# Summed weight tiles of a seven-product matmul: both of their transfers on GpSimd's queue, three units ahead

## The chip, the cores and the metric

The kernel runs on one core of one Trainium2 chip. The time is device microseconds of one execution. Three timed runs of the kernel before took 825.82, 832.07 and 833.29 us (median 832.07); a separate execution was recorded by the hardware profiler. Engines are named as in the profile: PE is TensorE (PEld its weight loads), DVE is VectorE, ACT is ScalarE, POOL is GpSimd, SP is SyncE, which issues most transfers.

## The reference

One layer of a decoder trunk on 256 tokens of width 2048, all in float32. What matters here is the order of the matrix products:

```
h  = rmsnorm(x)
u  = h @ w_in          # 12288 columns: conv fields, recurrence fields, then gates ga and gb (2048 columns each)
ya = short_conv(u);  yb = gated_recurrence(u)
m  = sigmoid(ga) * (ya @ w_a_out) + sigmoid(gb) * (yb @ w_b_out)
x  = x + m @ w_o
x  = x + sigmoid(rmsnorm(x) @ w_ple_gate) * (p @ w_ple_proj)
out = rmsnorm(x)
```

## The kernel before

Weights stream from DRAM once. Every weight tile (128 x 1024, two blocks of 512 columns) is cut into a high part (ScalarE copies it to float32r, line 160) and a low part (VectorE subtracts, line 161); a product is three matmuls, high by high, high by low, low by high (`triple`, lines 1021 to 1025). The main loop (line 1087 on) goes through a list of items, one per weight tile: projections of p, the fields of w_in, then for j = 0 to 3 the gate columns followed by four tiles each of w_a and w_b, then w_o, then the last gate. Items are split `LEAD` = 3 or more ahead of their matmuls and loaded `AHEAD` = 4 ahead; raw tiles have three buffers of two items each. Epilogues are generators of which each item advances one step.

For j = 1, 2, 3 the columns of ga and of gb, with two token halves and two halves of a 256-row chunk, form 2 x 2 block products. Of the eight chunks c, those in `SEVEN` (0, 2, 3, 5, 6) are done with seven products in place of eight (Strassen's scheme in Winograd's form); these are items of kind "S", called S units here (S0, S2, S3, S5, S6). Chunks 1, 4 and 7 are done plainly, as two items of kind "C" each. An S unit needs sums of weight blocks beside the blocks themselves:

- sA: the tile of ga (two blocks), which is also cut into whi and wlo and used as it is;
- sB: the second block of the tile of gb;
- sT: the tile of gb plus the first blocks of both tiles, added by the DMA engines: a plain load of the tile of gb (SP's queue, line 142) and then a load with `accum_op=add` (GpSimd's queue, line 143), which waits for the first.

`combine_weights` (line 176), called two items before the unit, adds sT and sB into sA on VectorE (line 691, twice) and cuts sT, sB and sA into thi/tlo, bhi/blo and thi/tlo. ScalarE's order for a unit is whi, thi (sT), bhi, thi (sA). thi and tlo have three buffers, bhi and blo one; sA, sB and sT have two each. `unit_products` (line 1050) issues the 21 matmuls, in the order x by the two halves of sA, then bhi/blo, then the summed weights. The sums on the token side are made once by `token_sums` (line 725), in three steps from w_a of j = 0 on, in scratch tiles `t4`.

All these lie in the pool "st", opened (`second_part`, line 967) with the scratch pool "tmp2" after the last gate item of j = 0, and closed when w_a of j = 3 begins (`parked`, line 1096). Then `unpark` (line 780) loads three stored tiles m into a pool "back" and cuts them; `ep_bb` (line 764) makes m for each j.

The order of instructions on each engine is the program's, with epilogue steps held behind the newest split; the queues of SP and of GpSimd are in order, and an issue that waits for a buffer or a transfer holds those behind it.

Of the kernel before, what the change touches and what calls it, by code (L numbers as in the profile page):

```python
# [9 lines left out]
F32 = mybir.dt.float32  # L10
F32R = mybir.dt.float32r
AF = mybir.ActivationFunctionType
ALU = mybir.AluOpType
PSUM = bass.MemoryType.PSUM

P = 128
# [7 lines left out]
CW = 512  # L24
# [23 lines left out]
def hybrid_kernel(ctx, tc, xT, x, pT, prm, gfin, masks, w_in, w_a, w_b, w_o, w_pg, w_pp, out):  # L48
    nc = tc.nc
# [9 lines left out]
    pools, closers = {}, {}  # L59
# [13 lines left out]
    state = {"tmp": "tmp1"}  # L73
# [3 lines left out]
    def nm(s):  # L77
        uid[0] += 1
        return f"{s}_{uid[0]}"

    def t4(tag="t4", bufs=None):
        bufs = bufs or {"tmp1": 8, "tmp2": 2, "tmp3": 5}[state["tmp"]]
        return pools[state["tmp"]].tile([P, 1024], F32, tag=tag, bufs=bufs, name=nm(tag))

    def bank(tag):
# [7 lines left out]
    loaded = {}  # L93
    parts = {}
    sums = {}

    groups = [("PP", j, w_pp, j, "pT") for j in range(4)]
    for n, (kind, j) in enumerate(IN_ORDER):
# [6 lines left out]
    items = []  # L105
    for gi, (kind, j, w, g, op) in enumerate(groups):
        if kind == "gb" and SEVEN[j]:
            continue
        for c in range(w.shape[2]):
            it = {"gi": gi, "kind": kind, "j": j, "c": c, "last": c == w.shape[2] - 1}  # L110
# [11 lines left out]
    def raw_of(pos):  # L122
        it = items[pos]
        if it["raw"] not in loaded:
            if it["kind"] == "S":
                t = tuple(
                    pools["st"].tile([P, n, CW], F32, tag=tag, bufs=2, name=nm(tag))
                    for tag, n in (("sA", 2), ("sB", 1), ("sT", 2))
                )
            else:  # L130
                t = wp.tile([P, 2, 2 * CW], F32, tag="raw", bufs=3, name=nm("raw"))
            loaded[it["raw"]] = t
        return loaded[it["raw"]]

    def load(pos):
        it = items[pos]
        if it["raw"] not in loaded:
            raw, (w, g, c) = raw_of(pos), it["w"]
            if it["kind"] == "S":
                A, B, X = raw  # L140
                for to, n, z in ((X, 1, 0), (A, 0, 0), (B, 1, 1)):
                    nc.sync.dma_start(out=to.rearrange("p n x -> p (n x)"), in_=w[g + n, :, c, z * CW :])
                nc.gpsimd.dma_start(  # L143
                    out=X, in_=w[g : g + 2, :, c, :CW].rearrange("n p x -> p n x"), accum_op=ALU.add
                )
            elif it["kind"] == "C":
                for n in range(2):
                    nc.sync.dma_start(out=raw[:, n, :], in_=w[g + n, :, c, :])
            elif pos < APART:
                for i in range(2):  # L150
                    w, g, c = items[pos + i]["w"]
                    nc.sync.dma_start(out=raw[:, i, :], in_=w[g, :, c, :])
            else:
                nc.sync.dma_start(out=raw, in_=w[g, :, c : c + 2, :])

    def pair_of(pool, n, tags=("whi", "wlo"), width=2 * CW):
        return tuple(pool.tile([P, width], F32R, tag=tag, bufs=n, name=nm(tag)) for tag in tags)

    def cut(hi, lo, src):
        a = nc.scalar.activation(out=hi, in_=src, func=AF.Copy)  # L160
        v = nc.vector.tensor_tensor(out=lo, in0=src, in1=hi.bitcast(F32), op=ALU.subtract)  # L161
        state["splits"] = (a.ins, v.ins)
# [12 lines left out]

    def combine_weights(pos):
        st = pools["st"]
        A, B, X = raw_of(pos)
        add(A[:, 0], X[:, 0], B[:, 0])
        add(A[:, 1], A[:, 0], A[:, 1])  # L180
        ts = []
        for n, src in enumerate((X, B, A)):
            hi, lo = pair_of(st, 1, ("bhi", "blo"), CW) if n == 1 else pair_of(st, 3, ("thi", "tlo"))
            cut(hi, lo, src.rearrange("p n x -> p (n x)"))
            ts += [(hi[:, i * CW : (i + 1) * CW], lo[:, i * CW : (i + 1) * CW]) for i in range(1 if n == 1 else 2)]
        t1, t3, b22, t2, t4_ = ts
        sums[pos] = (b22, t1, t3, t2, t4_)

    last_group = len(items) - w_pg.shape[2]
    gate = len(items) - 4 * w_pg.shape[2]  # L190
# [88 lines left out]
    def blocks(ap):  # L279

        return ap.rearrange("p (c b e) -> p c b e", b=4, e=32)
# [8 lines left out]
    def to_dram(src, tag, bufs):  # L290
        d = dram.tile([P, 4, T], F32, tag=tag, bufs=bufs, name=nm(tag))
        to = d.rearrange("(b i) a x -> a i b x", b=4)
        for a in range(4):
            nc.sync.dma_start(out=to[a], in_=src[32 * a : 32 * a + 32, :].rearrange("i (b x) -> i b x", b=4))
        return d
# [6 lines left out]
    def turned(src, lag, dst=None):  # L302
        d = to_dram(src, "turn", 3)
        yield
        nc.sync.dma_start(out=src, in_=d.rearrange("p a x -> p (a x)"))
        for _ in range(lag):
            yield
        dst = t4() if dst is None else dst
        square_turn(dst, src)
        return dst  # L310
# [379 lines left out]
    def add(out, a, b):  # L690
        nc.vector.tensor_tensor(out=out, in0=a, in1=b, op=ALU.add)  # L691
# [33 lines left out]
    def token_sums():  # L725
        nu = len(SEVEN[1])
        state["S"] = pair_of(pools["st"], 1, ("shi", "slo"), nu * 4 * P)
        state["S"] = tuple(v.rearrange("p (u s t) -> p u s t", u=nu, s=4) for v in state["S"])
        for first, n in TOGETHER:
            for _ in range(3):  # L730
                yield
            F, S = (t4()[:, : n * 4 * P] for _ in range(2))
            c = SEVEN[1][first]
            hi, lo = (v[:, 2 * c : 2 * (c + n), :] for v in state["hT"])
            Fv = F.rearrange("p (k t) -> p k t", t=T)
            nc.vector.tensor_tensor(out=Fv, in0=hi.bitcast(F32), in1=lo.bitcast(F32), op=ALU.add)
            yield
            Fv = F.rearrange("p (u r b t) -> p u r b t", u=n, r=2, b=2)
            Sv = S.rearrange("p (u s t) -> p u s t", u=n, s=4)
            a11, a12, a21, a22 = Fv[:, :, 0, 0], Fv[:, :, 1, 0], Fv[:, :, 0, 1], Fv[:, :, 1, 1]  # L740
            s1, s2, s3, s4 = (Sv[:, :, i] for i in range(4))
            for out, u, v, op in (
                (s1, a21, a22, ALU.subtract), (s2, s1, a11, ALU.subtract),
                (s3, a11, a21, ALU.subtract), (s4, a12, s2, ALU.add),
            ):
                nc.vector.tensor_tensor(out=out, in0=u, in1=v, op=op)
            hi, lo = (v[:, first : first + n] for v in state["S"])
            nc.scalar.activation(out=hi, in_=Sv, func=AF.Copy)
            nc.vector.tensor_tensor(out=lo, in0=Sv, in1=hi.bitcast(F32), op=ALU.subtract)
            yield  # L750
# [13 lines left out]
    def ep_bb(j, psum):  # L764
        ga, gb = state["ga"], state["gb"]
        for t in range(NT):
            s = slice(t * CW, (t + 1) * CW)
            nc.vector.tensor_tensor(out=gb[:, s], in0=gb[:, s], in1=psum[t], op=ALU.mult)  # L768
        m = t4()
        for t in range(NT):  # L770
            s = slice(t * CW, (t + 1) * CW)
            nc.vector.tensor_tensor(out=spread(m, t), in0=blocks(ga[:, s]), in1=blocks(gb[:, s]), op=ALU.add)
        if j == 3:
            m = yield from turned(m, 3)
            put_m(j, m)
        else:
            state["m", j] = to_dram(m, f"m{j}", 1)
            yield

    def unpark():  # L780
        def back():
            return pools["back"].tile([P, 1024], F32, tag="back", bufs=4, name=nm("back"))

        srcs = []
        for j in range(3):
            if j == 0:
                srcs = [back() for _ in range(2)]
                for i in range(2):
                    nc.sync.dma_start(out=srcs[i], in_=state["m", i].rearrange("p a x -> p (a x)"))
                yield  # L790
                yield
            if j == 2:
                srcs.append(back())
                nc.sync.dma_start(out=srcs[2], in_=state["m", 2].rearrange("p a x -> p (a x)"))
                yield
                yield
            m = back()
            square_turn(m, srcs[j])
            put_m(j, m)
            yield  # L800
# [286 lines left out]
    for pos, it in enumerate(items[:last_group]):  # L1087
        mark = len(nc.cur_bb.bb.instructions)
        kind, j, c, last = (it[n] for n in ("kind", "j", "c", "last"))
        _, _, w, g, opname = groups[it["gi"]]  # L1090
# [42 lines left out]
        if pos == NORM + 4:  # L1133
# [3 lines left out]
            for i in range(4):  # L1137
                z = slice(i * Q, (i + 1) * Q)
# [29 lines left out]
        if pos == begun:  # L1168
            finish()
            second_part()  # L1170
            active.append(token_sums())
        if kind == "O" and j == 0 and c == nch - 3:
            finish()
            third_part()
# [22 lines left out]
    for t, halves in ((0, (0, 1)), (1, (0,)), (1, (1,))):  # L1197
        bk, n = bank("g"), CW // 2
# [91 lines left out]
```

## Time and profile before

| | |
|---|---|
| timed runs, us | 825.82, 832.07, 833.29 |
| profiled execution, us | 828.21 |
| its span, us | 826.4 |
| mean granted TensorE clock | 0.992 |
| DMA traffic | 198.52 MB, mean 240 GB/s |
| q1 (SP's transfers) | 188.93 MB, 65.8% of 16 engines |
| q0 (GpSimd's transfers) | 7.87 MB, 5.6% of 16 engines |

The span runs from the first to the last instruction; the profiled execution's own time is 1.8 us longer. The S units of the three groups lie between about 435 and 615 us. In the profile's tables a row names a line, an engine and an operation with its tiles (out<-in); brackets in a timeline give the idle time before the instruction and what ended it. The windows view gives, for stretches of the span, busy time and number of instructions of each engine, the granted clock, the DMA engines' share and the rate. A landing is the time from a transfer's issue to its completion.

### The profile page before, as it was taken

How to read it: one execution, taken by the hardware profiler on the slowest of the kernel's cores; microseconds unless marked ns; L12 is line 12 of the kernel's file. 1: busy time of each engine (PE TensorE's matmuls, PEld its weight loads, DVE VectorE, ACT ScalarE, POOL GpSimd, SP SyncE). 2: the span in 40 equal slices, each digit the busy share in tenths (PEclk: the TensorE clock that was granted, in tenths of full speed). 3: DMA queues.
4: the chain of work that ended last, by engine and by line, in shares of the span. 5: the costliest groups of instructions: out<-in, count | busy, mean ns of one | idle time of the engine just before them, and what ended most of it. 6: DMA issues, size and time to landing. Idle time of an engine off the chain costs nothing.

```text
span 826.4 us, 10670 instructions
## 1 busy us (share of the span) xinstructions
PE 808.5 (98%) x4059; PEld 666.2 (81%) x4059; DVE 588.6 (71%) x745; ACT 458.6 (55%) x614; POOL 39.7 (5%) x42
## 2 busy tenths in 40 slices
PE   9999999999999999999999989999999999999995
PEld 6888888888888888888888868878877788888885
DVE  6756598767666588758678878688787756676932
ACT  7576466456464575475454555366455455566623
POOL 1000000010000000010000110110100000000210
PEclk9999999999999999999999989999999999999998
DMA  9998555648876555648888986997854888797712
GB/s 335 391 308 299 190 184 198 204 158 273 266 222 233 180 196 192 218 159 290 277 274 248 282 238 224 271 294 245 245 181 194 276 290 282 261 339 283 264 42 102
DMA packets 52659, 198.52 MB, mean 240 GB/s; under 512 B 6784, under 2 KB 16256, under 8 KB 37888
## 3 DMA queue, kind: packets, MB, share of 16 engines
q1 hardware_dynamic: 47952, 188.93, 65.8%
q0 software_dynamic: 4080, 7.87, 5.6%
q10 hardware_dynamic: 576, 1.05, 0.4%
q8 instruction: 31, 0.51, 0.2%
q14 instruction: 20, 0.16, 0.1%
HBM read 184.19 MB, written 13.63 MB: 239 GB/s over the span
## 4 chain that ended last, share of the span: by engine, by line
PE 76%; DVE 10%; DMA 7%; issue 4%; ACT 2%; POOLq 0%; POOL 0%; DVEq 0%; ACTq 0%
PE g L1023 24%; PE g L1024 24%; PE g L1025 24%; DMA sT<-in_w_in 6%; DVE wlo L161 4%; DVE tlo L161 2%; DVE sA L691 2%; ACT whi L160 1%; DMA raw<-in_w_o 1%; PE s L1024 1%; PE s L1025 1%; PE s L1023 1%; PE s L474 1%; DVE gb L768 0%; DVE back L298 0%
## 5 line engine op out<-in xcount | busy, mean ns | idle before, releaser
L161 DVE TENSOR_TENSOR wlo<-raw,whi 128x1024 fp32r<-128x1024 f32 (+1 forms) x264 | 319.9, 1227 | 160.8 <-ACT whi L160 158.9
L160 ACT ACTIVATE whi<-raw 128x1024 fp32r<-128x1024 f32 (+1 forms) x264 | 272.9, 1049 | 209.2 <-PE g L1025 175.4
L1024 PE MATMUL g<-wlo,xh 128*128 128x512 f32 (+1 forms) x738 | 283.7, 384 | 0.0
L1025 PE MATMUL g<-whi,xl 128*128 128x512 f32 (+1 forms) x738 | 283.6, 384 | 0.0
L1023 PE MATMUL g<-whi,xh 128*128 128x512 f32 (+1 forms) x738 | 283.5, 385 | 0.0
L1025 PEld LDWEIGHTS g<-whi,xl 128*128 128x128 f32 x738 | 138.6, 188 | 27.7
L1024 PEld LDWEIGHTS g<-wlo,xh 128*128 128x128 f32 x738 | 138.7, 188 | 27.6
L1023 PEld LDWEIGHTS g<-whi,xh 128*128 128x128 f32 x738 | 138.7, 188 | 27.1
L1024 PE MATMUL g<-wlo,mh 128*128 128x512 f32 x128 | 49.9, 390 | 0.2 <-DVE wlo L161 0.2
L1023 PE MATMUL g<-whi,mh 128*128 128x512 f32 x128 | 49.7, 389 | 0.0
L1025 PE MATMUL g<-whi,ml 128*128 128x512 f32 x128 | 49.5, 389 | 0.0
L160 ACT ACTIVATE thi<-sT 128x1024 fp32r<-128x1024 f32 x15 | 15.8, 1053 | 35.1 <-DMA sT<-in_w_in 35.1
L1024 PE MATMUL s<-wlo,xh 128*128 128x512 f32 x84 | 32.7, 389 | 0.0
L1025 PE MATMUL s<-whi,xl 128*128 128x512 f32 x84 | 32.7, 389 | 0.0
L1023 PE MATMUL s<-whi,xh 128*128 128x512 f32 x84 | 32.5, 391 | 0.0
L1024 PEld LDWEIGHTS g<-wlo,mh 128*128 128x128 f32 x128 | 24.0, 188 | 5.6 <-DVE wlo L161 0.7
L143 POOL DMA_DIRECT2D sT<-in_w_in x15 | 18.2, 1213 | 213.4 <-DMA sT<-in_w_in 69.5
L1023 PEld LDWEIGHTS g<-whi,mh 128*128 128x128 f32 x128 | 24.0, 188 | 5.1
L1025 PEld LDWEIGHTS g<-whi,ml 128*128 128x128 f32 x128 | 24.0, 188 | 5.0
L1024 PE MATMUL g<-wlo,ybTh 128*128 128x512 f32 x64 | 25.0, 391 | 1.0 <-DVE wlo L161 1.0
L160 ACT ACTIVATE thi<-sA 128x1024 fp32r<-128x1024 f32 x15 | 15.8, 1055 | 18.0 <-DVE sA L691 17.9
L1025 PE MATMUL g<-whi,ybTl 128*128 128x512 f32 x64 | 24.9, 389 | 0.0
(214 smaller groups left out, 917.5 us busy)
## 6 DMA issues: line engine op xcount, KB each, us to landing
raw<-in_w_in SPq DMA_DIRECT2D x66, 1024.0 KB, 5.0
raw<-in_w_o SPq DMA_DIRECT2D x16, 1024.0 KB, 7.0
raw<-in_w_pg SPq DMA_DIRECT2D x16, 1024.0 KB, 6.9
raw<-in_w_in SPq DMA_DIRECT2D x28, 512.0 KB, 5.3
raw<-in_w_a SPq DMA_DIRECT2D x8, 1024.0 KB, 7.8
raw<-in_w_b SPq DMA_DIRECT2D x8, 1024.0 KB, 7.0
turn<-t SPq DMA_DIRECT2D x60, 128.0 KB, 2.8
t<-turn SPq DMA_DIRECT2D x15, 512.0 KB, 5.2
```

What stands on the lines that cost most here:

```text
L143: nc.gpsimd.dma_start(out=X, in_=w[g : g + 2, :, c, :CW].rearrange("n p x -> p n x"), accum_op=ALU.add)
L160: a = nc.scalar.activation(out=hi, in_=src, func=AF.Copy)
L161: v = nc.vector.tensor_tensor(out=lo, in0=src, in1=hi.bitcast(F32), op=ALU.subtract)
L474: nc.tensor.matmul(out, X[:, 0, h, s], X[:, 1, h, t], start=True, stop=True, tile_position=(0, i * n))
L691: nc.vector.tensor_tensor(out=out, in0=a, in1=b, op=ALU.add)
L1023: nc.tensor.matmul(psum, oh, hi, start=first, stop=False)
L1024: nc.tensor.matmul(psum, oh, lo, start=False, stop=False)
L1025: nc.tensor.matmul(psum, ol, hi, start=False, stop=last)
```

## The change

Line numbers below are those of the kernel before.

- The plain load of sT leaves `load` (SP's queue) and the adding one goes with it into a new function `add_by_dma`, which issues both on GpSimd's queue for the next S unit that has none yet.
- It is called three times when the pool "st" is open, so that the first three units' transfers are issued there, and once at the end of each `combine_weights`, for the unit three further on. sT has three buffers in place of two.
- To make room, the scratch pool "tmp2" has one t4 in place of two; the token sums use buffers of thi and tlo for their scratch tiles; the m of j = 3 is turned into a tile of the pool "back", which has five buffers in place of four.

In the changed program the order of instructions on TensorE is that of before; on VectorE and ScalarE the order is that of before in the S units, but for tile names and waits. SP has 15 transfers fewer and GpSimd 15 more. GpSimd's list is: three plain loads, three adding ones, and from there in turn one plain load (it waits for VectorE's last read of the buffer) and its adding one (it waits for that load), to the fifteenth unit.

```diff
-        bufs = bufs or {"tmp1": 8, "tmp2": 2, "tmp3": 5}[state["tmp"]]
+        bufs = bufs or {"tmp1": 8, "tmp2": 1, "tmp3": 5}[state["tmp"]]
...
+    pair_sums = {}
...
                 t = tuple(
-                    pools["st"].tile([P, n, CW], F32, tag=tag, bufs=2, name=nm(tag))
-                    for tag, n in (("sA", 2), ("sB", 1), ("sT", 2))
+                    pools["st"].tile([P, n, CW], F32, tag=tag, bufs=2, name=nm(tag)) for tag, n in (("sA", 2), ("sB", 1))
                 )
...
             if it["kind"] == "S":
-                A, B, X = raw
-                for to, n, z in ((X, 1, 0), (A, 0, 0), (B, 1, 1)):
-                    nc.sync.dma_start(out=to.rearrange("p n x -> p (n x)"), in_=w[g + n, :, c, z * CW :])
-                nc.gpsimd.dma_start(
-                    out=X, in_=w[g : g + 2, :, c, :CW].rearrange("n p x -> p n x"), accum_op=ALU.add
-                )
+                for n, to in enumerate(raw):
+                    nc.sync.dma_start(out=to.rearrange("p n x -> p (n x)"), in_=w[g + n, :, c, n * CW :])
...
+    def add_by_dma():
+        pos = next((n for n, it in enumerate(items) if it["kind"] == "S" and n not in pair_sums), None)
+        if pos is not None:
+            w, g, c = items[pos]["w"]
+            X = pair_sums[pos] = pools["st"].tile([P, 2, CW], F32, tag="sT", bufs=3, name=nm("sT"))
+            nc.gpsimd.dma_start(out=X.rearrange("p n x -> p (n x)"), in_=w[g + 1, :, c, :])
+            nc.gpsimd.dma_start(out=X, in_=w[g : g + 2, :, c, :CW].rearrange("n p x -> p n x"), accum_op=ALU.add)
...
     def combine_weights(pos):
         st = pools["st"]
-        A, B, X = raw_of(pos)
+        (A, B), X = raw_of(pos), pair_sums[pos]
...
         sums[pos] = (b22, t1, t3, t2, t4_)
+        add_by_dma()
...
-            F, S = (t4()[:, : n * 4 * P] for _ in range(2))
+            F, S = (
+                pools["st"].tile([P, 2 * CW], F32R, tag=tag, bufs=3, name=nm(tag))[:, : n * 4 * P].bitcast(F32)
+                for tag in ("thi", "tlo")
+            )
...
         if j == 3:
-            m = yield from turned(m, 3)
+            m = yield from turned(m, 3, back())
...
+    def back():
+        return pools["back"].tile([P, 1024], F32, tag="back", bufs=5, name=nm("back"))
+
     def unpark():
-        def back():
-            return pools["back"].tile([P, 1024], F32, tag="back", bufs=4, name=nm("back"))
...
             active.append(token_sums())
+            for _ in range(3):
+                add_by_dma()
```

## The prediction

> **What bounds the kernel now.** I read the page first (busy time, chain of waits, groups), then waits by engine, the windows of 395 to 660 us in 5 us steps, and last the timelines of the five engines there.
>
> ```profile
> span 826.4 us, 10670 instructions
> ...
> PE 808.5 (98%) x4059; PEld 666.2 (81%) x4059; DVE 588.6 (71%) x745; ACT 458.6 (55%) x614; POOL 39.7 (5%) x42
> ...
> PE g L1023 24%; PE g L1024 24%; PE g L1025 24%; DMA sT<-in_w_in 6%; DVE wlo L161 4%; DVE tlo L161 2%; DVE sA L691 2%; ACT whi L160 1%; DMA raw<-in_w_o 1%; PE s L1024 1%; PE s L1025 1%; PE s L1023 1%; PE s L474 1%; DVE gb L768 0%; DVE back L298 0%
> ```
>
> TensorE is busy 98% of the span, so only about 18 us of it are idle. The chain gives 6% (50 us) to transfers of sT, but most of those 50 us lie beside busy matmuls: a late sT first eats the lead that the splits have over TensorE. What counts is where TensorE itself stops.
>
> ```profile
> PE s L1024 <- DVE blo L161: 3.7, 5, 1.0
> PE s L1023 <- ACT bhi L160: 2.7, 1, 2.7
> ...
> ACT thi L160 <- DMA sT<-in_w_in: 35.1, 8, 6.8
> ```
>
> ```profile
> 475.00:480.00 5.00, 1.31 (x5) 0.57 (x4) 3.52 (x5) 3.48 (x5) 1.19 (x1) 0.90 0.59 150
> 480.00:485.00 5.00, 5.00 (x13) 3.84 (x13) 5.00 (x5) 3.31 (x4) 0.00 (x0) 0.50 1.05 327
> ...
> 540.00:545.00 5.00, 4.20 (x18) 3.49 (x19) 4.93 (x7) 3.16 (x5) 0.38 (x1) 1.00 0.98 290
> ...
> 605.00:610.00 5.00, 4.96 (x21) 3.77 (x21) 4.93 (x6) 3.16 (x5) 0.00 (x0) 1.00 0.09 15
> ```
>
> Columns: stretch, then busy us of PE, PEld, DVE, ACT, POOL with counts, granted clock, DMA share, GB/s. TensorE waits for the pieces of an S unit (bhi, blo) 6 times, 3.7 + 2.7 = 6.4 us together, in one place of each of the three seven-product groups (near 475, 540, 605). Each time ScalarE's thi stands behind the summed weights of the fifth or fourth S unit, and bhi, the adds and blo stand behind thi. After the first stop the granted clock is 0.50 for 5 us.
>
> ```profile
> 474.84 0.39 PE L1024 MATMUL s<-wlo,xh 128*128 128x512 f32 x1
> 475.07 0.39 PE L1025 MATMUL s<-whi,xl 128*128 128x512 f32 x1
> 478.15 0.50 PE L1023 MATMUL s<-bhi,shi 128*128 128x512 f32 x1 [2.69 <-ACT bhi L160]
> 479.65 0.79 PE L1024 MATMUL s<-blo,shi 128*128 128x512 f32 x1 [1.00 <-DVE blo L161]
> 480.24 0.63 PE L1025 MATMUL s<-bhi,slo 128*128 128x512 f32 x1
> ...
> 485.79 0.42 PE L1023 MATMUL s<-whi,xh 128*128 128x512 f32 x1
> ```
>
> ```profile
> 539.54 0.39 PE L1023 MATMUL s<-bhi,shi 128*128 128x512 f32 x1
> 540.80 0.50 PE L1024 MATMUL s<-blo,shi 128*128 128x512 f32 x1 [0.87 <-DVE blo L161]
> ```
>
> A matmul normally follows after 0.23 us. From 480.24 to 485.79 there are 13 steps in 5.55 us where 13 x 0.23 = 2.95 would do: 2.6 us lost to the clock. A wait costs a little more than its length: 540.80 - 539.54 - 0.23 = 1.03 us for a wait of 0.87, so 0.16 more; six times, 1.0 us. **All that sT costs the matmuls is 6.4 + 2.6 + 1.0 = 10.0 us**, and this is the most that the change can win at this place.
>
> [...]
>
> **The change part by part.** Now the last sT of group one (unit S6), whose lateness causes the stop:
>
> ```profile
> 454.12 1.22 DVE L161 TENSOR_TENSOR tlo<-sT,thi 128x1024 fp32r<-128x1024 f32 x1
> 459.59 1.22 DVE L161 TENSOR_TENSOR tlo<-sT,thi 128x1024 fp32r<-128x1024 f32 x1
> 460.83 0.33 SPq L142 DMA_DIRECT2D sT<-in_w_in  x1
> 467.60 1.19 POOL L143 DMA_DIRECT2D sT<-in_w_in  x1 [6.87 <-DMA sT<-in_w_in]
> 471.14 1.22 DVE L161 TENSOR_TENSOR wlo<-sA,whi 128x1024 fp32r<-128x1024 f32 x1
> 476.44 0.69 DVE L691 TENSOR_TENSOR sA<-sT,sB 128x512 f32<-128x512 f32 x1 [4.08 <-issue]
> 478.91 0.68 DVE L161 TENSOR_TENSOR blo<-sB,bhi 128x512 fp32r<-128x512 f32 x1
> ```
>
> With two buffers, S6 takes S3's, free when its tlo ends (459.59 + 1.22 = 460.81); SP loads at 460.83, GpSimd adds at 467.60, and VectorE goes on at 476.44 instead of 471.14 + 1.22 = 472.36. With three buffers S6 takes S2's, free at 454.12 + 1.22 = 455.34, 5.5 us earlier. blo ends 478.91 + 0.68 - 476.44 = 3.15 us after the first add begins; unstalled, TensorE would need blo at 475.07 + 2 x 0.23 = 475.53. So **sT must be there by 472.4, 17.1 us after S2's buffer is free**.
>
> The new pair of transfers is the one term that the trace does not show: a plain load on GpSimd's queue, then the adding one, which waits for it.
>
> ```profile
> sT<-in_w_in SPq DMA_DIRECT2D x15, 512.0 KB, 5.5
> ...
> sT<-in_w_in POOLq DMA_DIRECT2D x15, 512.0 KB, 9.3
> ```
>
> The landings of SP's line 142 (sT, sA and sB together), then those of GpSimd's line 143:
>
> ```profile
> DMA to landing us min/median/max: 3.6/6.1/10.5
> ```
>
> ```profile
> L143 POOL DMA_DIRECT2D sT<-in_w_in x15: 1194/1203/1366, 403.8 to 597.3; - x15
> ...
> DMA to landing us min/median/max: 5.9/9.3/11.6
> ```
>
> Load: between SP's 3.6 and 10.5 us; I take 5.5, the median of the same bytes to the same tile. Add: unchanged, 5.9 to 11.6, median 9.3. With 0.5 for the semaphore between, an estimate, the chain takes 15.3 us (bounds 10.0 to 22.6), and S6's sT lands at 455.34 + 15.3 = 470.6, 1.8 us ahead of need. For the other two groups:
>
> ```profile
> 518.88 1.22 DVE L161 TENSOR_TENSOR tlo<-sT,thi 128x1024 fp32r<-128x1024 f32 x1
> ...
> 545.47 0.39 PE L1023 MATMUL s<-bhi,shi 128*128 128x512 f32 x1
> ```
>
> Free at 518.88 + 1.22 = 520.10; need: TensorE's blo at 545.47 - 1.03 + 0.23 = 544.7, less 3.15, is 541.5. That leaves 21.4 us for 15.3; group three repeats group two. S5 has more time still, since its buffer (S0's) comes free a unit pair earlier. So all three stops go: -10.0 us.
>
> GpSimd issues 15 more transfers: 15 x 1.2 = 18 us on an engine busy for 39.7 of 826.4, at nothing. Its queue is in order, so S5's add, waiting for its load, holds back S6's load.
>
> ```profile
> 440.18 1.22 DVE L161 TENSOR_TENSOR tlo<-sT,thi 128x1024 fp32r<-128x1024 f32 x1
> ```
>
> S5's chain starts when S0's tlo ends, 440.18 + 1.22 = 441.40, and its add is out by 441.40 + 5.5 + 0.5 + 1.2 = 448.6, ahead of S6's start at 455.34. If that cover went, S6's chain would start later by the overlap. SP loses 15 x 0.33 = 5 us of issues and its waits before sT; nothing in the chain hangs on SP there.
>
> The first three chains start when the pool is open, near 400, for a need after 435; they move S3's traffic into this stretch:
>
> ```profile
> 395.00:430.00 35.00, 35.00 (x156) 28.98 (x155) 23.21 (x27) 17.52 (x20) 2.58 (x2) 1.00 0.89 289
> ```
>
> The share of 0.89 leaves 11% of 35 us, 3.9 us, and the splits there wait for TensorE and not for weights, so nothing; uncovered, up to one pair's 4.6 us of DMA time (second rival) would meet a lead of three items. The token sums move into thi and tlo buffers, where the same engine writes and reads in order: nothing. One scratch buffer in place of two serves one m per group, stored long before the next: nothing. The fifth `back` buffer makes its loads wait for the last S unit's matmuls; that unit starts near 609 and has 21 x 0.23 = 4.8 us of them. The loads go out after it even now:
>
> ```profile
> 616.45 0.85 SPq L789 DMA_DIRECT2D back<-m  x2
> 627.00 2.60 SPq L154 DMA_DIRECT2D raw<-in_w_o  x2
> ```
>
> What is queued behind them on SP goes at 627: nothing, and up to 10 us later would still be covered. When the stops go, VectorE is late next: blo of S6 then ends at 472.36 + 3.15 = 475.5, just as TensorE comes to it.
>
> **Sum.** The profiled execution took 828.21 us (span 826.4); minus 10.0 is 818.2. It was 3.9 us faster than the median of the runs shown (832.07); from that the same step gives 822.1. I forecast the middle, 820, with a base of 830.
>
> **Rivals.** *Late in group one only.* The margin is 1.8 us. With a chain of 20 us S6 is 2.9 us late, stops TensorE as long as now and halves the clock again (2.9 + 2.6 + 0.2 = 5.7), while groups two and three stay clean: gain 4.3, 826. For it: both bounds' sum is 22.6. Against: the chain's parts are medians. Chance 0.18.
>
> *Moved traffic is no gain.* The pair competes with S6's own sA, issued behind it:
>
> ```profile
> 462.57 0.33 SPq L142 DMA_DIRECT2D sA<-in_w_in  x1
> ```
>
> ```profile
> q1 hardware_dynamic: 13049, 47.00, 61.3%
> q0 software_dynamic: 4080, 7.87, 20.9%
> ```
>
> In 395 to 615 the adds took 20.9% of 220 us over 15, 3.1 us of all engines each, and a plain load 0.52 / 47.00 of 61.3% of 220 us, 1.5 us. sA's own landings:
>
> ```profile
> DMA to landing us min/median/max: 4.1/6.6/8.8
> ```
>
> If an add goes ahead of sA, it lands at 462.57 + 8.8 + 3.1 = 474.5 at worst, TensorE stops as now, and the time stays 830. Against it: by the median alone sA is there at 469.2. Chance 0.10. [...]
>
> *Slower: GpSimd's queue is slower than any row.* If load and add take 24.2 us, S6 is 7.1 late in group one (7.1 + 2.6 + 0.2 = 9.9) and 2.8 late in the other two, each with a halved clock (5.6): 21.1 against 10.0 now, 841. It decides from 22.2 us on (7.9 + 1.0 + 1.0, as now). The longest landings seen make 22.6, so it needs both at their worst in every group. Chance 0.10.
>
> **How the numbers follow.** Forecast 0.62 (820), the rivals 0.18 (826), 0.10 (830), 0.10 (841). A measurement tells about 1% (8.3 us) from no change. Of the forecast's 0.62, whose 10.0 is just above that, three quarters count as faster, and a little of the first rival: 0.49 faster; 0.11 slower, from the last rival; 0.40 within 1%. The range leaves out the slower rival and little at the bottom: 812 (fastest run, 825.82, less 10.0, less another 3.9 by which executions differ) to 831.
>
> **What would show it.** Right: no wait of ScalarE's thi for sT, matmuls without a stop near 475, 540 and 605, clock 1.00 there, GpSimd's load issued right after the tlo of three units before, and a chain of about 15 us. Wrong: a chain over 17 us with TensorE waiting for bhi in the first group; weight loads or sA as the new last arrival; an idle TensorE near 615 to 630 behind `back`.

## The result and the profile after

The changed kernel took 818.19, 818.54, 817.41 and 818.57 us (median 818.37). The kernel before, on the same chip, took 825.82, 832.07, 833.29 and 832.19 (median 832.13). The ratio is 0.9855 with a 95% interval of 0.9811 to 0.9898: faster by about 1.5%, where 820 us had been forecast. The profiled executions are 10.0 us apart, 828.21 before and 818.19 after (spans 826.4 and 816.1, 10.3 apart). The kernel before was run another 37 times in three later sets, with medians of 826.33, 825.77 and 825.94; against those, the gain is 7.4 to 8.0 us. The changed kernel hardly moves (817 to 819 us in all runs), the kernel before does (823 to 834), so most of what is uncertain in the ratio is the kernel before.

The page of the changed kernel, busy time and the chain of work that ended last:

```profile
span 816.1 us, 10646 instructions
...
PE 804.2 (99%) x4059; PEld 664.6 (81%) x4059; DVE 589.0 (72%) x745; ACT 459.1 (56%) x614; POOL 49.2 (6%) x57
...
PE g L1033 26%; PE g L1034 26%; PE g L1032 26%; DVE wlo L165 3%; PE s L1033 2%; PE s L1034 2%; PE s L1032 2%; DMA sA<-in_w_in 1%; DMA raw<-in_w_pp 1%; DVE tlo L165 1%; ACT whi L164 1%; DMA raw<-in_w_o 1%; DVE sA L696 1%; PE s L479 1%; DVE back L303 0%
```

The transfers of sT, 6% of the chain before, are gone from these entries. Of the S units' transfers, sA is there now, with 1%. The waits of 395 to 650 us show the same; each row gives the total, the number and the longest in us:

```profile
POOL sT L158 <- DMA sT<-in_w_in: 86.1, 12, 13.3
...
ACT whi L164 <- DMA sA<-in_w_in: 3.5, 2, 2.7
...
PE s L1033 <- DVE blo L165: 1.1, 1, 1.1
```

ScalarE's thi waited for sT 8 times before (35.1 us) and does not wait for it once now. TensorE's six waits for the pieces of an S unit (6.4 us) have become one of 1.1. The 86.1 us in the first row are GpSimd's: the adding transfer waits for its load, and no engine waits for GpSimd in this stretch. The windows answer to the three of before (us, then busy time of each engine, granted clock, DMA share, GB/s); the later ones are shifted by what has been gained by then:

```profile
475.00:480.00 5.00, 3.86 (x17) 2.91 (x16) 4.97 (x7) 4.04 (x5) 0.00 (x0) 1.00 0.95 242
480.00:485.00 5.00, 5.00 (x23) 4.14 (x23) 4.96 (x6) 1.29 (x2) 1.78 (x2) 1.00 0.84 236
530.00:535.00 5.00, 5.00 (x24) 4.14 (x23) 4.74 (x7) 2.30 (x3) 1.74 (x2) 1.00 0.89 314
535.00:540.00 5.00, 5.00 (x24) 4.14 (x23) 3.69 (x4) 3.71 (x5) 0.04 (x1) 1.00 0.99 230
...
600.00:605.00 5.00, 5.00 (x24) 4.14 (x23) 5.00 (x5) 4.13 (x5) 0.00 (x0) 1.00 0.16 26
```

TensorE is full wherever it stopped before, but for 1.1 us in the first of these rows, and the clock stays at 1.00, after that stop too. Now unit S6 of the first group, the one whose sT was late. Its rows in the timeline of the changed kernel, in order of time (brackets: idle before, and what ended it):

```profile
454.96 1.22 DVE L165 TENSOR_TENSOR tlo<-sT,thi 128x1024 fp32r<-128x1024 f32 x1
456.48 0.60 POOL L157 DMA_DIRECT2D sT<-in_w_in  x1 [7.78 <-DVE tlo L165]
461.36 1.17 POOL L158 DMA_DIRECT2D sT<-in_w_in  x1 [4.28 <-DMA sT<-in_w_in]
462.07 1.05 POOL L157 DMA_DIRECT2D sT<-in_w_in  x1
463.40 0.33 SPq L141 DMA_DIRECT2D sA<-in_w_in  x1
472.09 1.06 ACT L164 ACTIVATE whi<-sA 128x1024 fp32r<-128x1024 f32 x1 [2.70 <-DMA sA<-in_w_in]
472.14 1.18 POOL L158 DMA_DIRECT2D sT<-in_w_in  x1 [9.01 <-DMA sT<-in_w_in]
473.06 1.04 ACT L164 ACTIVATE thi<-sT 128x1024 fp32r<-128x1024 f32 x1
476.13 0.39 PE L1032 MATMUL s<-bhi,shi 128*128 128x512 f32 x1
477.66 0.50 PE L1033 MATMUL s<-blo,shi 128*128 128x512 f32 x1 [1.14 <-DVE blo L165]
```

S2's tlo frees the buffer at 454.96 + 1.22 = 456.18; GpSimd loads at 456.48 and adds at 461.36, and the adding transfer lands 6.9 us later:

```profile
DMA to landing us min/median/max: 6.9/6.9/6.9
```

So sT is whole at 468.3, 12.1 us after its buffer came free, and 4.8 us before ScalarE cuts it at 473.06, without a wait. The last to come is now sA: issued at 463.40, cut at 472.09 after a wait of 2.70. From its cut on, everything of S6 is late by that much less the lead, and TensorE stops once, 477.66 - 476.13 - 0.23 = 1.30 us. Why sA comes so late is the prediction's question asked of another tile: its buffer is the one that S3's sA had, VectorE's last read of that ends at 463.38 (a tlo of 1.22 us from 462.16), and SP issues the load at 463.40. sA has two buffers; a third one was not tried.

### The profile page after: what moved, and what is told of

Read it like the earlier page. It is cut to its first block, busy times and chain, and to the rows that moved or that the text cites. A ratio compares the mean times of both kernels' runs of the same rounds, so it can differ in the third digit from the quotient of the medians.

```text
span 816.1 us, 10646 instructions
## 1 busy us (share of the span) xinstructions
PE 804.2 (99%) x4059; PEld 664.6 (81%) x4059; DVE 589.0 (72%) x745; ACT 459.1 (56%) x614; POOL 49.2 (6%) x57
## 4 chain that ended last, share of the span: by engine, by line
PE 85%; DVE 7%; issue 3%; DMA 3%; ACT 2%; POOLq 0%; POOL 0%; DVEq 0%; ACTq 0%
PE g L1033 26%; PE g L1034 26%; PE g L1032 26%; DVE wlo L165 3%; PE s L1033 2%; PE s L1034 2%; PE s L1032 2%; DMA sA<-in_w_in 1%; DMA raw<-in_w_pp 1%; DVE tlo L165 1%; ACT whi L164 1%; DMA raw<-in_w_o 1%; DVE sA L696 1%; PE s L479 1%; DVE back L303 0%
## 5 line engine op out<-in xcount | busy, mean ns | idle before, releaser
L1032 PE MATMUL g<-whi,yaTh 128*128 128x512 f32 x64 | 24.9, 389 | 0.0
L1033 PE MATMUL g<-wlo,yaTh 128*128 128x512 f32 x64 | 24.9, 389 | 0.0
```

The lines of the kernel that those rows point to most:

```text
L1032: nc.tensor.matmul(psum, oh, hi, start=first, stop=False)
L1033: nc.tensor.matmul(psum, oh, lo, start=False, stop=False)
```

## The experiments

The theory from the prediction: the time hung on the buffer. A third one lets S6's transfers start 5.5 us earlier, and that is the gain; which queue carries the plain load matters little. The rival: the queue matters, because transfers on one queue keep their order (in the trace of the changed kernel S6's add, issued at 461.36, lands at 468.3, and the load of 462.07 behind it on GpSimd's queue at 471.9). A second question came with the profile after: why sA is late there.

All times are the changed kernel's with one edit, unless said otherwise; ratios are to the kernel before, run beside it. Each run left one profiled execution, so a trace is one case and the timed runs say how typical it is.

**Two buffers in place of three, both transfers on GpSimd's queue.**

```diff
-            X = pair_sums[pos] = pools["st"].tile([P, 2, CW], F32, tag="sT", bufs=3, name=nm("sT"))
+            X = pair_sums[pos] = pools["st"].tile([P, 2, CW], F32, tag="sT", bufs=2, name=nm("sT"))
...
-            for _ in range(3):
+            for _ in range(2):
                 add_by_dma()
```

> The changed kernel with two buffers of sT in place of three, and two units ahead in place of three; both transfers stay on GpSimd's queue. Buffer theory (the third buffer lets the pair of transfers start one unit sooner, and this is the gain): the last unit's pair starts only when the third unit's tlo ends, some 5 us later, the stops of TensorE near 475, 540 and 600 us come back at least in part, 822 to 829 us. Queue theory (what counts is that the plain load no longer stands in SP's queue): no stop, 818 us as with three buffers.

Measured: 833.51 us (828.09 to 836.15), ratio 1.0067 (1.003 to 1.0104). That is beyond the 822 to 829 of the buffer theory. In the trace the stops of the first two groups are back and longer: TensorE loses 5.26 + 1.44 us near 481 and 3.40 + 1.44 near 551, and the clock is halved (0.50 in 480 to 485; 0.986 in the mean of the execution, where the changed kernel had 0.997); the third group has no stop. In the timeline of this kernel, the buffer's release, S5's add, S6's load, S6's add and the cut:

```profile
459.50 1.22 DVE L165 TENSOR_TENSOR tlo<-sT,thi 128x1024 fp32r<-128x1024 f32 x1
460.05 1.18 POOL L158 DMA_DIRECT2D sT<-in_w_in  x1 [3.90 <-DMA sT<-in_w_in]
461.01 0.81 POOL L157 DMA_DIRECT2D sT<-in_w_in  x1
471.38 1.17 POOL L158 DMA_DIRECT2D sT<-in_w_in  x1 [9.56 <-DMA sT<-in_w_in]
479.63 1.06 ACT L164 ACTIVATE thi<-sT 128x1024 fp32r<-128x1024 f32 x1 [8.00 <-DMA sT<-in_w_in]
```

The load goes out a moment after S5's add on the same queue, and S6's add cannot be issued before 471.38, 10.4 us later; with the kernel before's SP queue that step took 467.60 - 460.83 = 6.8. From the release at 460.72 to the cut it is 18.9 us. Without the third buffer the move to GpSimd's queue loses 0.7%; the gain needs the buffer.

**Three buffers, the plain load on SP's queue as before.**

```diff
-            nc.gpsimd.dma_start(out=X.rearrange("p n x -> p (n x)"), in_=w[g + 1, :, c, :])
+            nc.sync.dma_start(out=X.rearrange("p n x -> p (n x)"), in_=w[g + 1, :, c, :])
```

> The changed kernel with the plain load of sT back on SP's queue, still three units ahead with three buffers. Buffer theory: 818 to 821 us, since SP issues the last unit's load some 2 us later than GpSimd did, within the margin. Queue theory: the stops come back, 826 to 830 us.

Measured: 822.0 us (819.0 to 822.69), ratio 0.9924 (0.9894 to 0.9953). S6 in its timeline:

```profile
458.59 0.38 SPq L157 DMA_DIRECT2D sT<-in_w_in  x1
463.93 1.19 POOL L158 DMA_DIRECT2D sT<-in_w_in  x1 [16.13 <-DMA sT<-in_w_in]
464.02 0.38 SPq L157 DMA_DIRECT2D sT<-in_w_in  x1
476.07 1.06 ACT L164 ACTIVATE thi<-sT 128x1024 fp32r<-128x1024 f32 x1 [6.01 <-PE s L1034]
477.70 0.50 PE L1032 MATMUL s<-bhi,shi 128*128 128x512 f32 x1 [1.66 <-ACT bhi L164]
479.19 0.79 PE L1033 MATMUL s<-blo,shi 128*128 128x512 f32 x1 [1.00 <-DVE blo L165]
```

Two things are later than with GpSimd's queue. SP comes to the load at 458.59, behind its own transfers of sA and sB, where GpSimd issued it at 456.48. And the adding transfer takes 12.0 us in place of 6.9:

```profile
DMA to landing us min/median/max: 12.0/12.0/12.0
```

The brackets at 476.07 name TensorE, but the add lands at 463.93 + 12.0 = 475.9, and that is what released the cut. The next unit's load goes out on SP at 464.02, right beside the add. In the changed kernel the same load was issued at 462.07, behind the add on its own queue, and it was that load which took 9.8 us, while the add took 6.9. sA has changed sides too: here it goes out at 463.12, ahead of the add, and lands after 3.8 us; in the changed kernel it went out behind the add and took 8.7. Which of these neighbours costs the add its 5.1 us was not tried apart.

So the buffer alone gives part of the gain (about 4 us of time by medians), and the queue the rest. The intervals of the two ratios overlap (the changed kernel once more, below: 0.9855 to 0.9927); the times hardly do, 819.0 to 822.69 here with five of six above 821, and 817.03 to 819.39 for all ten runs of the changed kernel. In the two traces TensorE loses 1.82 and 1.26 us in a row near 478 here, with a halved clock after it (0.50 from 478.6 to 482.0), and 1.27 near 543, against 1.30 in all there.

**The plain load twice**, to lengthen the chain by a known transfer; the margin in groups two and three was put at 6 us.

```diff
-            nc.gpsimd.dma_start(out=X.rearrange("p n x -> p (n x)"), in_=w[g + 1, :, c, :])
+            for _ in range(2):
+                nc.gpsimd.dma_start(out=X.rearrange("p n x -> p (n x)"), in_=w[g + 1, :, c, :])
```

> The changed kernel with the plain load of sT issued twice, one after the other, ahead of the adding one (the sums stay what they are): every chain is one landing, 5 to 6 us, longer and moves half a megabyte more. Threshold theory (only the chain of the first group's last unit against the 17 us that it has): it grows from 12 to about 17 us, TensorE's stop in the first group becomes 1 to 2 us longer, none in the others, 819 to 822 us. Traffic theory (what the queues move sets the time): 7.9 MB more in the same stretch bring stops in all three groups, 826 us or more.

Measured: 845.32 us (839.25 to 846.66), ratio 1.0193 (1.0144 to 1.0242). The threshold theory's 819 to 822 was far off; the traffic theory's signs, stops in all three groups and over 826 us, are there. Load, second load, add and cut of S6:

```profile
461.25 0.57 POOL L158 DMA_DIRECT2D sT<-in_w_in  x1 [3.44 <-DVE tlo L166]
467.76 1.05 POOL L158 DMA_DIRECT2D sT<-in_w_in  x2 [5.94 <-DMA sT<-in_w_in]
474.30 1.22 POOL L159 DMA_DIRECT2D sT<-in_w_in  x1 [5.48 <-DMA sT<-in_w_in]
483.46 1.06 ACT L165 ACTIVATE thi<-sT 128x1024 fp32r<-128x1024 f32 x1 [8.15 <-DMA sT<-in_w_in]
```

The steps take 6.5, 6.5 and 9.2 us, where the changed kernel had 4.9 and 6.9: one more transfer does not only add its own time, the others are longer too. The edit also changed the order on GpSimd's queue: the second row stands for two loads, and the later one (468.28) is the next unit's, which in the changed kernel went out behind S6's add. The chain is 22.2 us from the first load to the cut, TensorE stops in all three groups (4.15, 5.62 and 4.74 us before bhi, 1.4 us more before blo each time), and the granted clock falls:

```profile
485.00:490.00 5.00, 4.04 (x9) 2.85 (x10) 5.00 (x5) 4.98 (x7) 1.77 (x2) 0.50 0.65 103
```

The length of these stops is what the prediction's need times say. From the release of the buffer to the landing, S6's chain takes 22.4, 28.1 and 27.2 us in the three groups. Less the 17.1 and 21.4 us that the prediction found there (group three as group two), sT is 5.3, 6.7 and 5.8 us late, and the two stops of each group sum to 5.6, 7.1 and 6.2. So both theories hold a part: how late sT is sets the stops, and what else the queues move, or in which order, made it later than the sum of its own parts. It is the state that the prediction's slower rival described, 841 us for chains of 24.2, brought about here by an added transfer.

**The room-making edits alone**, on the kernel before: one scratch tile, token sums in thi and tlo, five buffers for `back`.

```diff
-        bufs = bufs or {"tmp1": 8, "tmp2": 2, "tmp3": 5}[state["tmp"]]
+        bufs = bufs or {"tmp1": 8, "tmp2": 1, "tmp3": 5}[state["tmp"]]
...
-            F, S = (t4()[:, : n * 4 * P] for _ in range(2))
+            F, S = (
+                pools["st"].tile([P, 2 * CW], F32R, tag=tag, bufs=3, name=nm(tag))[:, : n * 4 * P].bitcast(F32)
+                for tag in ("thi", "tlo")
+            )
...
-            m = yield from turned(m, 3)
+            m = yield from turned(m, 3, back())
...
-            return pools["back"].tile([P, 1024], F32, tag="back", bufs=4, name=nm("back"))
+        return pools["back"].tile([P, 1024], F32, tag="back", bufs=5, name=nm("back"))
```

> The kernel before with only what makes room: one scratch buffer in place of two, the token sums in buffers of thi and tlo, five buffers of back. If these cost and gain nothing, 828 to 833 us and the same three stops as before. If they have a share in the result, the time moves by 2 us or more from the kernel before on the same chip.

Measured: 825.84 us (822.49 to 831.1), ratio 0.9995 (0.9968 to 1.0021). TensorE's waits for the pieces of S units, 395 to 660 us:

```profile
PE s L1028 <- DVE blo L161: 4.2, 5, 1.0
PE s L1027 <- ACT bhi L160: 2.8, 2, 2.6
```

7.0 us in 7 waits against 6.4 in 6: within 0.3%, these edits neither gain nor lose. The long one (2.6) lies in group three here and in group one in the profile of the kernel before; whether the edits move it or one execution differs from the next, two profiles cannot tell.

**The adding transfers left out**; the sums are then not formed, and sT holds the plain tile.

```diff
-            nc.gpsimd.dma_start(out=X, in_=w[g : g + 2, :, c, :CW].rearrange("n p x -> p n x"), accum_op=ALU.add)
```

> The changed kernel without the adding transfers, so that sT holds the tile of gb alone and the sums are not formed. It shows what sT could still give: if the adds' traffic costs what is left, no stop in the three groups and 816 to 817.5 us; if nothing of it is left, the changed kernel's time.

Measured: 816.59 us (816.48 to 817.25), ratio 0.9875 (0.9823 to 0.9927); the changed kernel, once more beside it, took 818.17 (817.03 to 819.39), ratio 0.9891 (0.9855 to 0.9927). The stop near 476 is gone, and S6's sA, issued at 462.7, lands after

```profile
DMA to landing us min/median/max: 4.9/4.9/4.9
```

in place of 8.7. With the adds gone, only 1.6 us are left to gain here by medians.

> The changed kernel as it is, timed beside the other kernels of this job: 0.985 to 0.990 of the kernel before, one stop of TensorE of about 1.3 us near 476 us.

Measured: 818.17 us, ratio 0.9891, and in its trace one stop of 1.25 us behind 476.61, with sA landing after 8.6 us: as expected.

**Later transfers for the next group.** GpSimd loads the first sum of the next group at 462.07, just ahead of sA. This edit asks for it one unit later in the program, at the sums of S5 in place of S3's. (Its expectation speaks of the fifth unit; the edit does not do that, since S5, the fourth, still asks for one pair.)

```diff
-        add_by_dma()
+        for _ in range({3: 0, 6: 2}.get(items[pos]["c"], 1)):
+            add_by_dma()
```

> The changed kernel, but the pair of transfers for the next group's first unit is issued at the fifth unit's sums in place of the third's (two pairs are asked for there). In the changed kernel that pair goes out 1.3 us ahead of the last unit's sA, which then lands after 8.7 us. Contention theory (this pair delays sA, and sA makes the stop that is left): sA lands in 5 to 7 us, the stop near 476 us goes, 1 to 2 us less than the changed kernel. Own-issue theory (sA is late because its own buffer comes free late): the stop stays, same time as the changed kernel.

Measured: 818.57 us (817.5 to 820.59), ratio 0.9898 (0.9861 to 0.9935). It does not decide between the theories: GpSimd issued the load at 462.13 all the same, right behind S6's add at 461.41, 0.4 us after its buffer came free (460.56 + 1.22 = 461.78). GpSimd has no other instruction between the two places in the program, so the move changed nothing for it. The trace is thus one more of the changed kernel's schedule: sA lands after 8.3 us, and the stop is 0.91.

**The same, held by a wait.** GpSimd copies one column of S6's whi into the buffer ahead of that load. The copy waits for ScalarE's cut of S6's sA.

```diff
+            if behind is not None:
+                nc.gpsimd.tensor_copy(out=X[:, 0, :1], in_=behind[:, :1].bitcast(F32))
             nc.gpsimd.dma_start(out=X.rearrange("p n x -> p (n x)"), in_=w[g + 1, :, c, :])
...
-        add_by_dma()
+        for i in range({3: 0, 5: 0, 6: 3}.get(items[pos]["c"], 1)):
+            add_by_dma(parts[pos][0] if items[pos]["c"] == 6 and i == 0 else None)
```

> The changed kernel, with the load of the next group's first sum held back on GpSimd until the last unit of this group has its sA (a copy of one column on GpSimd, which waits for ScalarE's cut of that sA, stands ahead of the load). In the changed kernel that load goes out at 462.1 us, the last unit's sA at 463.4, and sA lands 8.7 us later; ScalarE waits 2.7 us for it and TensorE stands still for 1.1 to 1.3 us near 476. Theory 1 (the load made the sA late, by sharing the DMA engines with it): sA lands in 5 to 7 us, ScalarE's wait for it goes, the stop near 476 goes, 816.5 to 817.5 us. Theory 2 (sA is late because of the adding transfer of its own unit, which still runs beside it, or because it is issued so late): sA still takes about 8 us, the stop stays, 818 to 819 us. A third way: the next group's sums, now some 10 us later, are late themselves, and a stop comes at the start of the next group, above 819 us.

Measured: 817.08 us (816.33 to 818.48), ratio 0.9894 (0.9874 to 0.9914). GpSimd's copy and the loads behind it, SP's issue and ScalarE's cut of sA, and TensorE's blo:

```profile
464.49 0.33 SPq L141 DMA_DIRECT2D sA<-in_w_in  x1
472.20 1.06 ACT L166 ACTIVATE whi<-sA 128x1024 fp32r<-128x1024 f32 x1 [1.73 <-DMA sA<-in_w_in]
473.33 1.24 POOL L158 COPY sT<-whi 128x1 f32<-128x1 f32 x1 [9.52 <-ACT whi L166]
474.51 1.15 POOL L159 DMA_DIRECT2D sT<-in_w_in  x2
477.77 0.50 PE L1036 MATMUL s<-blo,shi 128*128 128x512 f32 x1 [0.17 <-DVE blo L167]
```

The load is really held now, and sA lands in 7.7 us in place of 8.3 to 8.7 in the three traces without the wait. The stop shrinks to 477.77 - 477.22 - 0.23 = 0.32 us, from 0.91 to 1.30 there. Theory 1 was too simple: the load costs sA at most 1.0 of the 3.8 us that sA needs beyond the 4.9 of the kernel without adds. The rest goes with the adds. Which of them was not tried, but the trace of the load on SP's queue points at S6's own, which is issued ahead of sA here and in the changed kernel: all adds are in place there, S6's goes out 0.8 us behind sA, and sA lands after 3.8 us. The next group loses nothing: there is no stop between 478 and 648 us. Whether the time gains is not shown. By medians it is 1.1 us, but the two kernels ran on different chips, their ratios to the kernel before are alike (0.9894 and 0.9891), and their runs overlap (816.33 to 818.48 and 817.03 to 819.39).

## Why the prediction was right

The time, 818.4, is 1.6 us under the forecast, inside its range. The mechanism is the one forecast: S6's sums start one buffer earlier, and the stops for them go. Several terms of the sum were off and partly cancelled. Step by step:

- *All that sT costs the matmuls is 10.0 us.* It was more. Matching each matmul of the profile before with the same one after gives the loss directly. These two start at 475.07 and 485.79 before, ahead of the first stop and behind the half clock:

```profile
475.90 0.39 PE L1034 MATMUL s<-whi,xl 128*128 128x512 f32 x1
480.96 0.39 PE L1032 MATMUL s<-whi,xh 128*128 128x512 f32 x1
```

  From 0.8 us behind, the changed kernel is 4.8 ahead, and behind the third group's stops 9.0 ahead (611.40 and 602.45). So the S units gained 9.8 us. Some 1.4 us remain near 476, for sA, so the stops had cost 11.2, not 10.0: the 0.16 us that a wait was taken to cost beyond its length is 0.27 or 0.28 in two of the six, and the matmuls right behind the waits lose a little more.
- *What was not foreseen.* The prediction did not count one stop of the kernel before, further on:

```profile
638.16 0.61 PE L1023 MATMUL g<-whi,ybTh 128*128 128x512 f32 x2
639.78 0.50 PE L1024 MATMUL g<-wlo,ybTh 128*128 128x512 f32 x1 [1.01 <-DVE wlo L161]
```

  The first row stands for two matmuls 0.22 us apart, so the stop costs 639.78 - 638.38 - 0.23 = 1.17 us; the changed kernel has none there (at 629). The room-making edits alone do not show it either, and with two buffers it is there, so it need not be the change that removes it; what sets it was not tried. By the same matching, the 10.3 us between the spans are 9.8 in the S units and 1.3 here, less the 0.8 by which the changed kernel was behind at 475 (0.6 of it by 136 us, long before anything that was changed).
- *The third buffer frees S6 5.5 us earlier.* Shown: in the changed kernel's own trace S2's buffer comes free at 456.18 and S3's at 460.42 + 1.22 = 461.64, and with two buffers and the same queue the gain turns into a loss (1.0067).
- *The chain takes 15.3 us (bounds 10.0 to 22.6).* It took 12.1 here: load 4.9 with its semaphore for 6.0, add 6.9 for 9.3. The 0.5 for the semaphore rested on no row shown; in the profile before, S6's add goes out 0.6 us after the load has landed (460.83 + 6.2 and 467.60), here 0.3 us after (456.48 + 4.6 and 461.36). With the load on SP, where its medians were taken, the chain is 475.9 - 455.9 = 20.0 (S2's tlo there begins at 454.7 and takes 1.22). That is the first rival, in its own numbers: 2.9 us late (the two stops there are 1.82 + 1.26), the clock halved again, and a gain of 4.3 (826.33 to 822.0); only group two does not stay clean, it stops for 1.27. The 15.3 was a sum of medians from another queue. That it came out on the good side was not foreseen: the add landed in 6.9 us with the next load behind it on GpSimd's queue, and in 12.0 with that load on SP's.
- *GpSimd issues 15 more transfers for 18 us, at nothing.* A plain issue costs 0.6 us by the median (0.54 to 1.07), half of what was taken from the adding one; busy time rose by 49.2 - 39.7 = 9.5 us. At nothing is right: no row of the waits of 395 to 650 us names GpSimd as what an engine waited for. S5's add was out before S6's load, as worked out.
- *The first three chains start near 400, at nothing.* They start at 367.5, as soon as GpSimd gets to them, and fill the DMA engines:

```profile
365.00:400.00 35.00, 35.00 (x155) 28.76 (x154) 23.11 (x39) 18.30 (x27) 7.97 (x7) 1.00 1.00 325
```

  A share of 1.00 where it was 0.79 before. The splits' lead covered it but for 0.2 us near 390 (0.4 to 0.6 in the three later traces that begin in the same way; the kernel before loses nothing there). With one load more per sum it no longer did: TensorE stops near 389 and 410, and the matmul that starts at 448.99 here starts at 453.77 there.
- *Room-making edits at nothing.* Shown: 0.9995 (0.9968 to 1.0021).
- *When the stops go, VectorE is late next: blo of S6 ends just as TensorE comes to it.* Not so: sA is late next, by 2.70 us. The prediction had this as a rival ("moved traffic is no gain") and worked out sA's landing at 8.8 + 3.1 us at worst. 8.7 was measured (6.7 in the kernel before), and it costs 1.3 us, not the whole gain. The second rival was real, at about an eighth of its price.
- *The first rival: 2.9 us late halves the clock again.* From what length on a stop does that, the profile before does not show: it has 0.50 from 479.0 on, in the second of two waits of 2.69 and 1.00 us, and 1.00 behind one of 0.87. The stops of 1.30 (changed kernel) and 0.32 (held by a wait) left the clock at 1.00, so the forecast lost nothing here. In the trace of the room-making edits the granted clock is 0.50 from 602.8 on, behind one wait of 2.60 us, from 600.0 to 602.61, and before the next wait begins.

```profile
600.00:605.00 5.00, 1.55 (x4) 0.98 (x4) 4.07 (x5) 4.02 (x5) 0.00 (x0) 0.78 0.54 104
```

  With the load on SP it is 0.50 from 478.6 on, during the second of two waits of 1.66 and 1.00 us with a single matmul between them.

```profile
480.00:485.00 5.00, 5.00 (x19) 3.99 (x19) 5.00 (x6) 2.86 (x4) 0.00 (x0) 0.80 1.05 281
```

  Stops of 1.27 near 471 and 0.39 + 1.26 near 478 (room-making edits) left the clock at 1.00. No run varied the length of a stop alone.
- *The base.* The forecast took 830 as the time before. Its medians in four sets of runs are 832.13, 826.33, 825.77 and 825.94; only the profiled pair (828.21 to 818.19) has its 10.0 us exactly. From a base of 826 the same step would have given 816; that 820 came so near to 818.4 is in part luck, a base too high for most executions and a gain too large for them. The changed kernel lands at 818 in every set and the one before anywhere from 823 to 834. That stops halve the clock in some of its executions and not in others is an estimate from the clocks: of the 37 executions of the kernel before in the three later sets, the eight of up to 825 us had a mean granted clock of 0.995 to 0.998, the six from 829 us on 0.987 to 0.994, and the changed kernel had 0.996 to 0.998 in all of its runs. Which stops fell where in those executions was not recorded.

## What to carry to other kernels

Ask of a late transfer when its buffer came free, before asking how long it takes: one more buffer moved the start by some 5 us and gave about half of the gain by itself, where the same move of queues without it lost 0.7%. Work out, too, by when each transfer must be there: late by 2.9, 5.3, 6.7 and 5.8 us in the traces above, S6's sT stopped TensorE for 3.1, 5.6, 7.1 and 6.2. Look at the order of issue: with the transfer that nobody is waiting for behind the urgent one on its queue the add took 6.9 us, beside it on another 12.0; sA had changed sides too, and which of them did it was not tried apart. Moving its issue to a later line held nothing back where no other instruction of that engine stood between; a wait did. An estimate of a chain from medians needs the traffic beside it: the same load and add took about 12, 19 and 20 us in three arrangements.

## What was not expected of the hardware

Landings of the plain loads and of the adding transfers on GpSimd's queue, in the changed kernel (15 each):

```profile
DMA to landing us min/median/max: 4.6/5.9/14.1
```

```profile
DMA to landing us min/median/max: 6.3/8.4/19.2
```

After the first three, four plain loads were alone on the queue, or all but alone (issued at 442.5, 456.5, 505.4 and 567.3), and landed in 4.6 to 4.8 us. Two issued 5 us behind an add (515.5 and 577.4) took 5.6 and 5.9, and the six right behind an add (462.1, 472.9, 481.0, 522.1, 534.0 and 543.5) 7.1 to 14.1. The longest add, 19.2 us, is one of the three issued together near 375, beside the weight loads of that stretch. With one transfer more per sum (the load twice) S6's load and add took 1.6 and 2.3 us longer, so a transfer's time in a full stretch is no constant to be added up. The half clock lasted 6.8 us in the kernel before (479.0 to 485.8) and with the room-making edits (602.8 to 609.6), and 3.4 with the load on SP's queue (478.6 to 482.0).
